# A hybrid encoder layer on one core: stores moved from ScalarE to GpSimd, first input pieces in other tiles, a later residual load

## The chip, the core and the metric

The kernel runs on one core of a Trainium2 chip. The core has TensorE (PE in the profile; its weight loads are PEld), VectorE (DVE), ScalarE (ACT), GpSimd (POOL) and SyncE (SP), which here only issues DMAs. Each engine takes its instructions in its own order and waits on semaphores for the others. SBUF holds the tiles, PSUM the results of matmuls (eight banks of 128 x 512 f32), and larger arrays lie in DRAM. The metric is the device time of one execution in microseconds (us), the median of several.

## What is computed

One layer of a bidirectional encoder in float32: 2048 positions, width 1024. Cut to what matters here:

```python
u = rms_norm(x); proj = u @ w_in                       # 1024 -> 3600 columns
hy = conv3(proj[:, :1536])                             # v, x1, x2, 512 channels each
z, g1, g2 = hy                                         # Hyena: two long convolutions
for o, gate in enumerate((g1, g2)):
    conv = irfft(rfft(z, 2 * L) * spec[:, o])[:L]      # spec from a small sine network
    z = gate * (conv + z * skip[o])
qk = silu(conv3(proj[:, 1536:2560]))                   # mLSTM: 4 heads of 128, two directions
y_ml = sigmoid(o_pre) * (mlstm(q, k, v, gates) + flipped)
h = x + concat(group_norm(z), group_norm(y_ml)) @ w_out
h = h + cross_attention(rms_norm(h), rms_norm(mem))    # 256 memory rows, 4 heads
h = h + square(relu(rms_norm(h) @ w1)) @ w2            # 1024 -> 4096 -> 1024
return rms_norm(h)
```

## The kernel before

All large products are made in three matmuls: each operand is split into a rounded part and its remainder (`split`, L368, one ScalarE and one VectorE instruction), and `mm3` multiplies high x high (L357), high x low (L360) and low x high (L361). They write the four PSUM banks called `mm`. The long convolutions, filters and mLSTM steps use the other four, called `hy`.

The program is one list of instructions, and a planner (`schedule_with_timeline_sim`) puts each engine's part in order by a model of the times. Where the source says `behind(ins)`, the planner places `ins` after the last product made so far; no semaphore comes of it. `weave(a, b, wa, wb)` alternates two parts of the program: each `yield n` adds n to its part's account, and the part with the smaller account over its weight goes on.

The stages up to the attention, in the order of time:

- **Projection** (`sweep` and `natural`). `sweep` makes 128 columns by 512 positions per product (`yield 5.5`), leaves them in tiles P (L789), applies the short convolution in tiles cv (L797 to L802) and stores the turned result into the arrays hy, qt, kt and kn. `natural` makes the value, output gate and mLSTM gate columns (eight row blocks per 256 columns): ScalarE moves the bank into a staging tile st (L892, L894; three buffers, two row blocks each) and issues the store into vd or od (L897). For the gates VectorE adds the bias into sg (L900; two buffers of 128 x 16), and SyncE stores it into gt (L901), once per row block, sixteen times.
- **Filters** (`filters`), woven into the sweeps, in a pool of their own (`f_sb`). The matrix f1 (128 x 64) is loaded there. `front` stores the filter spectra into the arrays fs (L339). When the filters are done the pool closes, and the pool `h_sb` of the Hyena part is laid over the same memory: ten tiles `a` of 128 x 1024, five tiles b, and f1 once more, loaded again (L931).
- **Hyena** (`hyena`), woven with the rest of the projection at weights 329 and 445. First `load1` fetches a piece of hy in four DMAs (L938) into a tile `a`, for eight pieces; `spectrum(0, ...)` turns each by sixteen small matmuls over four hy banks (`beside`, L173 and L186), ScalarE and VectorE copy the banks out (L997), and the two halves are stored into zs (L339): one from ScalarE's queue, one from SyncE's. Then per block i: load of zs and fs (L918), matmul by dm (L955 for the filter, L1029 for the data), the complex product with ScalarE (L1031, L1032), VectorE (L1033, L1035) and GpSimd (L1034), matmul by em (L986), copy to gs (L987) and store into zg from ScalarE's queue (L988, 64 of them). Then `load3` reads zg and the gate rows (L339, L973), the last small matmuls follow, and VectorE multiplies by the gate (L1050). All this runs twice (o = 0, 1); for o = 0 the result goes through `spectrum(1, ...)`, for o = 1 it is normed on VectorE and GpSimd (L1059 to L1065) and stored into yh (L1067).
- **Backward mLSTM states** (`states`): load of va (L1183), weighting on GpSimd (L1195), matmul L1199, update L1205, store.
- **Memory products** (`memproj`), beside the first mLSTM steps: `project` (L709, copied by L711) and `keys` (L726) or `values` (L738), whose banks ScalarE copies into staging tiles st (L716) and stores from its own queue into gd (L728) and vw (L740).
- **mLSTM and attention.** At its start attention reads yh and ym rows, turns them on TensorE (L1478) and splits them (L368); `residual` (L1507) loads the 1 MB halves of x into acc. The mLSTM step reads va too (L1183) and weights it on ScalarE (L1193).

After the attention comes the feed-forward part to the end; nothing of the change lies there. The small pool `i_sb` holds, among others, two tiles xn of 128 x 1024, used by `row_stats` near the start and by the memory loads later.

Of the kernel before, what the change touches and what calls it, by code (L numbers as in the profile page):

```python
# [10 lines left out]
F32 = mybir.dt.float32  # L11
# [117 lines left out]
class Prog:  # L129
# [102 lines left out]
    def filters(self):  # L232
# [1 line left out]
        sd = [self.dram(f"fs{o}", (16, 64, 4, CH)) for o in range(2)]  # L234
        sb, ta, tb = self.fsb, self.ta, self.tb
        if True:
            fw, hid, f1 = self.f_w, self.f_hid, self.f_f1
            nc.sync.dma_start(out=fw, in_=a["fw"])
            w1, w2, w3 = fw[0:66, 0:128], fw[:, 128:256], fw[:, 256:1280].rearrange("p (o c) -> p o c", o=2)
            par = self.par[:, 128:132]  # L240
# [100 lines left out]
    def filters_open(self):  # L341
        self.fes = ExitStack()
        self.fsb = self.fes.enter_context(self.tc.tile_pool(name="f_sb", bufs=1))
        self.fsb.tile([128, 32], F32, name="f_even")
        self.f_w = self.fsb.tile([128, 1280], F32, name="fw")
        self.f_hid = self.fsb.tile([128, 16, 128], F32, name="hid")
        self.f_f1 = self.fsb.tile([128, 128], F32, name="f1")[:, 0:64]

    def ta(self):
        return self.fsb.tile([128, 2, CH], F32, tag="a", name="a", bufs=7)  # L350
# [77 lines left out]
    def inproj_open(self, es):  # L428
        nc, tc, a = self.nc, self.tc, self.a
        self.d_hy = self.dram("hy", (3, L, CH))  # L430
        self.d_qt = self.dram("qt", (4, 128, L))
        self.d_kt = self.dram("kt", (4, 128, L))
        self.d_kn = self.dram("kn", (L, CH))
        self.d_vd = self.dram("vd", (L, CH))
        self.d_od = self.dram("od", (L, CH))
        self.d_gt = self.dram("gt", (L, 16))
        sw = self.isw = es.enter_context(tc.tile_pool(name="i_w", bufs=1))
        for tag, n, bufs in (("cv", 1088, 2), ("wn", 544, 4)):
            for _ in range(bufs):
                sw.tile([128, n], F32, tag=tag, name=tag, bufs=bufs)  # L440
        self.ist = es.enter_context(tc.tile_pool(name="i_st", bufs=1))
        sb = self.isb = es.enter_context(tc.tile_pool(name="i_sb", bufs=1))
        self.xin = ExitStack()
        xp = self.xin.enter_context(tc.tile_pool(name="x_sb", bufs=1, side="right"))
        self.xh = xp.tile([128, 8, 1024], F32R, name="xh")
        self.xl = xp.tile([128, 8, 1024], F32R, name="xl")
        xp.tile([128, 56], F32, name="x_even")
        small = sb.tile([128, 448], F32, name="small")
        self.carry = small[:, 0:340].rearrange("p (c t) -> p c t", c=20)
        self.rx, self.rm = small[:, 340:356], small[:, 356:358]  # L450
        win = a["w_in"][0]
        tr = [(win[:, 256 * c:256 * c + 256], 256) for c in range(10)]
        nat = [(win[:, 2560 + 256 * c:2816 + 256 * c + 16 * (c == 3)], 256 + 16 * (c == 3)) for c in range(4)]
        hs = [slice(256 * h, 256 * h + 256) for h in range(4)]
        first = [(a[w][0][:, h], 256) for w in ("xa_wk", "xa_wv") for h in hs]
        second = [(a["xa_wq_t"][h, :], 1024) for h in hs] + [(a["xa_wo"][0][h, :], 1024) for h in hs]
        mem = first[:1]
        for i in range(8):
            mem += first[i + 1:i + 2] + second[i:i + 1]
        items = tr[:4] * 2 + tr[4:] + [nat[c] for c in (3, 0, 1, 2, 3)]  # L460
        items += [tr[c] for c in (4, 5, 8, 9)] + nat[:2] + tr[6:8] + nat[2:3]
        self.items, self.mem_items = items, mem
# [231 lines left out]
    def memproj(self):  # L694
# [24 lines left out]
        def keys(h, t):  # L719
            q = next(self.mst)  # L720
            for i2 in range(4):
                p = self.mm().rearrange("p (i t) -> p i t", i=2)
                for i in range(2):
                    ds = slice(256 * i2 + 128 * i, 256 * i2 + 128 * i + 128)
                    for m in range(2):
                        mul(p[:, i], q[:, m, ds], t[:, m], start=m == 0, stop=m == 1)  # L726
                cs = slice(256 * (h % 2), 256 * (h % 2) + 256)
                nc.scalar.dma_start(out=gd[h // 2, :, 2 * i2:2 * i2 + 2, cs], in_=staged(p))  # L728

        def values(h, t):  # L730
            o_ = next(self.mst)
            for mt in range(2):
                ms = slice(128 * mt, 128 * mt + 128)
                for d in range(2):
                    ds = slice(512 * d, 512 * d + 512)
                    p = self.mm()
                    for m in range(2):
                        mul(p, t[:, m, ms], o_[:, m, ds], start=m == 0, stop=m == 1)  # L738
                    o = staged(p.rearrange("p (i t) -> p i t", i=2))
                    nc.scalar.dma_start(out=vw[2 * d:2 * d + 2, :, 2 * h + mt].rearrange("i p c -> p i c"), in_=o)  # L740

        t = project()
        for i in range(8):
# [117 lines left out]
    def natural(self, hf, tiles, after=None, at=4):  # L861
# [3 lines left out]
        for c2 in tiles:  # L865
# [3 lines left out]
            for t in range(8):  # L869
# [24 lines left out]
                    nc.scalar.activation(so, p[:, :256], AF.Sigmoid)  # L894
                if t % 2:
                    dst = (self.d_vd if c2 < 2 else self.d_od)[r0 - 128:r0 + 128, 256 * (c2 % 2):256 * (c2 % 2) + 256]
                    nc.scalar.dma_start(out=dst.rearrange("(t p) c -> p t c", p=128), in_=st)  # L897
                if c2 == 3:
                    sg = sb.tile([128, 16], F32, tag="sg", name="sg", bufs=2)
                    nc.vector.tensor_tensor(sg, p[:, 256:272], self.gb, ALU.add)  # L900
                    nc.sync.dma_start(out=self.d_gt[r0:r0 + 128], in_=sg)  # L901

    def hyena(self, es):
        nc, tc, a = self.nc, self.tc, self.a
# [18 lines left out]
        def ta():  # L923
            return sb.tile([128, 2, CH], F32, tag="a", name="a", bufs=10)
# [1 line left out]
        def tb():  # L926
            return sb.tile([128, CH], F32, tag="b", name="b", bufs=5)

        f1 = sb.tile([128, 128], F32, name="f1")[:, 0:64]
        e2 = sb.tile([128, 64], F32, name="e2")[:, 0:32]  # L930
        nc.sync.dma_start(out=f1, in_=a["c_f1"])  # L931
        nc.sync.dma_start(out=e2, in_=a["c_e2"])
        ghy = self.bcast(sb, a["hy_norm_g"], CH, "ghy")
        def load1(j2):
            z = ta()
            js = slice(2 * j2, 2 * j2 + 2)
            for q in range(4):
                nc.sync.dma_start(out=z[phase[q]], in_=hy[0, q, :, js])  # L938
            return z
# [44 lines left out]
        def back(m, i, em, y, gs, dst):  # L984
            pg = self.hy()
            nc.tensor.matmul(pg, em[:, m], y, start=True, stop=True)  # L986
            nc.scalar.copy(gs[:, m], pg)  # L987
            nc.scalar.dma_start(out=of_block(dst, i, m), in_=gs[:, m])  # L988

        def spectrum(o, j2, z):  # L990
            st = [ta() for h in range(2)]
# [4 lines left out]
                for h in range(2):  # L996
                    (nc.vector.tensor_copy if h else nc.scalar.copy)(st[h][:, i], pp[2 * h + i])  # L997
            for h in range(2):
                self.by_phase(nc.sync if h else nc.scalar, sds[o], j2, h, st[h])

        q, fq = [load1(0), load1(1)], []
        yield 52
        self.strict = True
        for j2 in range(8):
            yield 3.5
            if j2 < 6:
                q.append(load1(j2 + 2))
            else:
                fq.append(load_filter(0, j2 - 6))
            spectrum(0, j2, q.pop(0))  # L1010
# [426 lines left out]
    def attention(self, es):  # L1437
# [65 lines left out]
        for c in range(4):  # L1503

            def residual(h):
                src = a["x_t"].rearrange("(k p) t -> p k t", p=128)[:, 4 * h:4 * h + 4, 512 * c:512 * c + 512]
                nc.sync.dma_start(out=acc[:, 4 * h:4 * h + 4], in_=src)  # L1507

            ssum = A.tile([128, 512], F32, tag="ssum", name="ssum", bufs=2)

# [679 lines left out]
```

## Time and profile before

| what | value |
|---|---|
| median of three runs | 3098.77 us (3090.32 to 3103.11) |
| profiled execution, its own time | 3100.22 us |
| its span, first to last instruction | 3098.5 us |
| mean granted clock of TensorE | 0.984 |
| DMA queue of SyncE | 407012 packets, 546.46 MB |
| DMA queue of ScalarE | 37380 packets, 57.79 MB |
| DRAM read, written | 401.70 MB, 202.41 MB |

How to read the rows shown below. A stretch (window) row gives the busy time of each engine between two times, the clock that TensorE was granted (1.00 is full), the share of the sixteen DMA engines' time and what they moved. A row of waits names the engine, the tile it writes and its line, what ended the wait, and then the total, the number of times and the longest, in us. A row of one line or tile gives the shortest, median and longest instruction in ns, and the first and last start. In timeline and chain rows the first number is the start and the second the length; in the chain a DMA's length is the time from its issue until what waited for it could go on. SPq and ACTq are the DMA queues of SyncE and ScalarE.

### The profile page before, as it was taken

The numbers are of one execution on the slowest core, as the hardware profiler recorded it, in microseconds if no ns is written. First come the engines' busy times: TensorE is split into PE (matmuls) and PEld (weight loads), VectorE is DVE, ScalarE is ACT, GpSimd is POOL, SyncE is SP. The second block draws the span as 40 slices with busy tenths as digits, with TensorE's granted clock in tenths as the row PEclk, the third lists the DMA queues.
The fourth block names the chain that finished last, engine by engine and source line by source line (L and its number), as shares of the span: only waits on it lengthen the run. The fifth ranks groups of instructions, "written<-read, shape, count | busy, mean of one in ns | idle before, by whom it ended". The sixth has DMA issues, their size and how long they took to land.

```text
span 3098.5 us, 44022 instructions
## 1 busy us (share of the span) xinstructions
PE 2989.6 (96%) x14799; PEld 2371.5 (77%) x14799; DVE 1945.6 (63%) x3442; ACT 1494.4 (48%) x2930; POOL 1121.0 (36%) x798
## 2 busy tenths in 40 slices
PE   9999899999999898999999999999999999999998
PEld 7666566776577676888888888888888888888876
DVE  8855365547745445877664666557555686566695
ACT  6443356534744235565544465556555543333335
POOL 0111012200222333333132336766466375344653
PEclk9999999999999999999999999999999999999999
DMA  6555578586767996465476556657544565354434
GB/s 223 188 191 175 198 238 250 181 268 201 241 212 217 315 303 195 152 200 167 150 245 217 188 185 226 209 179 241 196 153 151 179 213 175 110 165 119 155 102 163
DMA packets 444618, 607.06 MB, mean 196 GB/s; under 512 B 39262, under 2 KB 249054, under 8 KB 443368
## 3 DMA queue, kind: packets, MB, share of 16 engines
q1 hardware_dynamic: 407012, 546.46, 55.0%
q10 hardware_dynamic: 37380, 57.79, 5.5%
q8 instruction: 117, 1.92, 0.3%
q14 instruction: 109, 0.89, 0.1%
HBM read 401.70 MB, written 202.41 MB: 195 GB/s over the span
## 4 chain that ended last, share of the span: by engine, by line
PE 81%; DMA 9%; DVE 6%; issue 2%; ACT 1%; SPq 1%; POOL 0%; ACTq 0%; DVEq 0%; POOLq 0%
PE mm L357 17%; PE mm L361 17%; PE mm L360 17%; PE hy L357 6%; PE hy L361 6%; PE hy L360 6%; PE hy L173 2%; PE hy L1029 2%; PE hy L986 2%; PE mm L955 2%; DMA a<-zg 1%; PE mm L709 1%; PE hy L1321 1%; DMA xt<-in_x_t_dram 1%; PE hy L1323 1%
## 5 line engine op out<-in xcount | busy, mean ns | idle before, releaser
L1689 ACT CAST ah<-w 128x512 fp32r<-128x512 f32 x284 | 176.6, 623 | 302.1 <-PE hy L360 157.0
L1690 DVE TENSOR_TENSOR bl<-wr,bh 128x512 fp32r<-128x512 f32 x213 | 240.8, 1135 | 126.5 <-ACT bh L1689 126.4
L368 DVE TENSOR_TENSOR wl<-wn,wh 128x512 fp32r<-128x512 f32 (+1 forms) x296 | 215.7, 773 | 101.2 <-ACT wh L368 101.2
L357 PE MATMUL mm<-xh,wh 128*128 128x512 f32 x640 | 267.2, 419 | 3.2 <-ACT st L201 1.4
L360 PE MATMUL mm<-xl,wh 128*128 128x512 f32 x640 | 258.0, 403 | 4.5 <-DVE xl L368 4.4
L1034 POOL TENSOR_TENSOR b<-b,a 128x512 f32<-128x512 f32 x64 | 87.1, 1362 | 481.4 <-ACT b L1032 240.1
L361 PE MATMUL mm<-xh,wl 128*128 128x512 f32 x640 | 257.6, 403 | 0.0
L1689 ACT CAST bh<-wr 128x512 fp32r<-128x512 f32 x232 | 143.6, 621 | 229.9 <-PE mm L361 171.3
L1690 DVE TENSOR_TENSOR al<-w,ah 128x512 fp32r<-128x512 f32 x236 | 214.6, 910 | 55.1 <-ACT ah L1689 55.1
L361 PE MATMUL mm<-bh,al 128*128 128x512 f32 x576 | 224.1, 392 | 4.1 <-DVE al L1690 4.1
L357 PE MATMUL mm<-bh,ah 128*128 128x512 f32 x576 | 226.2, 393 | 0.5 <-DVE acc L1851 0.4
L360 PE MATMUL mm<-bl,ah 128*128 128x512 f32 x576 | 225.1, 391 | 0.0
L368 ACT CAST wh<-wn 128x512 fp32r<-128x512 f32 (+1 forms) x296 | 164.7, 620 | 105.4 <-PE mm L361 50.1
L360 PE MATMUL mm<-act,wh 128*128 128x512 f32 x512 | 201.9, 394 | 0.0
L357 PE MATMUL mm<-act,wh 128*128 128x512 f32 x512 | 199.4, 396 | 1.0 <-ACT wh L368 0.9
L361 PE MATMUL mm<-act,wl 128*128 128x512 f32 x512 | 199.6, 392 | 0.0
L357 PE MATMUL hy<-bh,ah 128*128 128x512 f32 x448 | 175.2, 391 | 0.0
L360 PE MATMUL hy<-bl,ah 128*128 128x512 f32 x448 | 174.6, 390 | 0.0
L361 PE MATMUL hy<-bh,al 128*128 128x512 f32 x448 | 174.4, 390 | 0.0
L357 PEld LDWEIGHTS mm<-xh,wh 128*128 128x128 f32 x640 | 122.4, 191 | 58.2 <-issue 24.3
L360 PEld LDWEIGHTS mm<-xl,wh 128*128 128x128 f32 x640 | 122.8, 192 | 47.4 <-issue 16.3
L357 PE MATMUL mm<-wh,xh 128*128 128x256 f32 (+1 forms) x512 | 157.4, 307 | 0.5 <-ACT st L894 0.5
(380 smaller groups left out, 8077.8 us busy)
## 6 DMA issues: line engine op xcount, KB each, us to landing
wr<-hc SPq DMA_DIRECT2D x224, 256.0 KB
w<-in_ff_w_dram SPq DMA_DIRECT2D x172, 256.0 KB
hc<-wn SPq DMA_DIRECT2D x128, 256.0 KB
wn<-in_w_in_dram SPq DMA_DIRECT2D x100, 256.0 KB
hc<-q SPq DMA_DIRECT2D x96, 256.0 KB
fs<-a SPq DMA_DIRECT2D x32, 512.0 KB
a<-fs SPq DMA_DIRECT2D x64, 256.0 KB
a<-zs SPq DMA_DIRECT2D x64, 256.0 KB
```

What stands on the lines that cost most here:

```text
L173: b = self.nc.tensor.matmul(*products[-1], start=True, stop=True)
L357: first = mm(ps, lh, rh, start=start, stop=False)
L360: mm(ps, lh, rl, start=False, stop=False)
L361: self.last = mm(ps, ll, rh, start=False, stop=stop)
L368: both = (self.nc.scalar.copy(hi, src), self.nc.vector.tensor_tensor(lo, src, hi.bitcast(F32), ALU.subtract))
L709: mul(p[:, m], w[:, k, ms], mt[k // 4][:, k % 4], start=k == 0, stop=k == 7)
L955: nc.tensor.matmul(pp, dm[:, m], t[:, m], start=True, stop=True)
L986: nc.tensor.matmul(pg, em[:, m], y, start=True, stop=True)
L1029: nc.tensor.matmul(pp, dm[:, m], t[:, m], start=True, stop=True)
L1034: nc.gpsimd.tensor_tensor(xt, xt, hi[:, m], ALU.mult)
L1689: self.nc.scalar.copy(hi, src)
L1690: eng.tensor_tensor(lo, src, hi.bitcast(F32), ALU.subtract)
```

## The change

```diff
 filters:
-            fw, hid, f1 = self.f_w, self.f_hid, self.f_f1
+            fw, hid, f1 = self.f_w, self.f_hid, self.f1
 filters_open:
-        self.fsb.tile([128, 32], F32, name="f_even")
-        self.f_f1 = self.fsb.tile([128, 128], F32, name="f1")[:, 0:64]
 inproj_open:
+        self.f1 = sb.tile([128, 64], F32, name="f1")
 memproj, keys and values:
-                nc.scalar.dma_start(out=gd[...], in_=staged(p))
+                nc.gpsimd.dma_start(out=gd[...], in_=staged(p))
-                    nc.scalar.dma_start(out=vw[...], in_=o)
+                    nc.gpsimd.dma_start(out=vw[...], in_=o)
 natural:
-                    nc.scalar.dma_start(out=dst.rearrange("(t p) c -> p t c", p=128), in_=st)
+                    nc.gpsimd.dma_start(out=dst.rearrange("(t p) c -> p t c", p=128), in_=st)
                 if c2 == 3:
-                    sg = sb.tile([128, 16], F32, tag="sg", name="sg", bufs=2)
-                    nc.vector.tensor_tensor(sg, p[:, 256:272], self.gb, ALU.add)
-                    nc.sync.dma_start(out=self.d_gt[r0:r0 + 128], in_=sg)
+                    if t == 0:
+                        sg = sb.tile([128, 8, 16], F32, tag="sg", name="sg", bufs=1)
+                    nc.vector.tensor_tensor(sg[:, t], p[:, 256:272], self.gb, ALU.add)
+                    if t == 7:
+                        dst = self.d_gt[1024 * hf:1024 * hf + 1024]
+                        nc.sync.dma_start(out=dst.rearrange("(t p) g -> p t g", p=128), in_=sg)
 hyena:
-        f1 = sb.tile([128, 128], F32, name="f1")[:, 0:64]
+        f1 = self.f1
-        nc.sync.dma_start(out=f1, in_=a["c_f1"])
 load1:
-            z = ta()
+            z = ta() if j2 > 1 else self.isb.tile([128, D], F32, tag="xn", name="z", bufs=2).rearrange("p (j c) -> p j c", j=2)
 back:
-            nc.scalar.dma_start(out=of_block(dst, i, m), in_=gs[:, m])
+            nc.gpsimd.dma_start(out=of_block(dst, i, m), in_=gs[:, m])
 spectrum:
-                self.by_phase(nc.sync if h else nc.scalar, sds[o], j2, h, st[h])
+                self.by_phase(nc.sync if h else nc.gpsimd, sds[o], j2, h, st[h])
 the eight pieces of spectrum(0, ...):
-            yield 3.5
+            yield 4.2
 attention, residual:
-                nc.sync.dma_start(out=acc[:, 4 * h:4 * h + 4], in_=src)
+                d = nc.sync.dma_start(out=acc[:, 4 * h:4 * h + 4], in_=src)
+                if c == 0:
+                    self.behind(d)
```

f1 is loaded once, into the small pool, and read by the filters and by Hyena. The first two pieces that Hyena reads lie in the two tiles xn; the other six in tiles `a`, as before. All stores that ScalarE issued in `natural`, `memproj`, `back` and `spectrum` are issued by GpSimd. The gates of eight row blocks are gathered in one tile and stored by one DMA per half of the positions. The eight pieces of the first spectrum weigh 4.2 in the weave, where they weighed 3.5. The first chunk's residual loads stand behind the last product made before them.

More of the change, by code (lines that the diff above doesn't have):

```diff
@@ L727, in keys @@
                 cs = slice(256 * (h % 2), 256 * (h % 2) + 256)
-                nc.scalar.dma_start(out=gd[h // 2, :, 2 * i2:2 * i2 + 2, cs], in_=staged(p))
+                nc.gpsimd.dma_start(out=gd[h // 2, :, 2 * i2:2 * i2 + 2, cs], in_=staged(p))
         def values(h, t):
@@ L739, in values @@
                     o = staged(p.rearrange("p (i t) -> p i t", i=2))
-                    nc.scalar.dma_start(out=vw[2 * d:2 * d + 2, :, 2 * h + mt].rearrange("i p c -> p i c"), in_=o)
+                    nc.gpsimd.dma_start(out=vw[2 * d:2 * d + 2, :, 2 * h + mt].rearrange("i p c -> p i c"), in_=o)
         t = project()
```

## Prediction

> **What bounds the kernel now.** I read the page's busy times first, then the stretches by stage, then what TensorE waited for, then single waits in the timeline.
>
> ```profile
> PE 2989.6 (96%) x14799; PEld 2371.5 (77%) x14799; DVE 1945.6 (63%) x3442; ACT 1494.4 (48%) x2930; POOL 1121.0 (36%) x798
> ```
>
> TensorE works 96% of the span, and the change removes no matmul. What can be won is its 109 us of idle time and the time in which its clock is down. The stretches show where that is (columns: stretch, its length, busy us and count of PE, PEld, DVE, ACT, POOL, then granted clock, DMA share, GB/s):
>
> ```profile
> 350.00:430.00 80.00, 64.61 (x337) 43.05 (x336) 32.60 (x51) 33.97 (x55) 0.00 (x0) 0.87 0.80 275
> 430.00:640.00 210.00, 205.43 (x1136) 153.15 (x1135) 124.79 (x194) 129.77 (x231) 42.79 (x32) 0.99 0.71 217
> 640.00:760.00 120.00, 105.72 (x657) 74.78 (x657) 70.67 (x155) 44.53 (x76) 3.84 (x2) 0.93 0.76 242
> 760.00:1020.00 260.00, 248.96 (x1279) 183.68 (x1278) 160.51 (x323) 142.00 (x240) 62.77 (x48) 0.99 0.74 225
> 1020.00:1120.00 100.00, 86.18 (x445) 69.60 (x444) 44.50 (x143) 23.60 (x56) 38.06 (x32) 0.93 0.96 311
> 1120.00:1210.00 90.00, 77.54 (x391) 58.28 (x390) 45.86 (x152) 43.32 (x147) 24.94 (x20) 0.92 0.78 260
> 1900.00:3098.00 1198.00, 1178.29 (x5245) 974.32 (x5243) 762.29 (x989) 539.42 (x934) 670.85 (x462) 0.99 0.52 169
> ```
>
> Between 350 and 1210 us, where every edit acts, PE is idle 71.6 us (860 less the six busy times); in the 1198 us of the feed-forward stage, which no edit touches, 19.7. The waits of PE name the causes (us in total, times, longest):
>
> ```profile
> PE hy L173 <- DMA a<-hy: 11.7, 1, 11.7
> PE hy L1478 <- DVE act L368: 9.1, 1, 9.1
> PE mm L726 <- ACT kt L711: 7.6, 2, 3.9
> PE hy L173 <- ACT a L997: 5.4, 2, 3.7
> PE hy L173 <- DVE a L1050: 5.3, 2, 4.6
> PE hy L986 <- DVE b L1035: 4.5, 2, 2.4
> ```
>
> Each long one also lowers the clock behind it. Pairs of ten-microsecond stretches around four of them, same columns:
>
> ```profile
> 350.00:360.00 10.00, 0.97 (x4) 0.45 (x3) 5.09 (x7) 6.85 (x11) 0.00 (x0) 0.73 0.92 319
> 360.00:370.00 10.00, 7.33 (x32) 4.68 (x33) 1.29 (x2) 1.08 (x2) 0.00 (x0) 0.59 0.89 255
> 390.00:400.00 10.00, 6.30 (x45) 2.99 (x44) 8.31 (x14) 7.03 (x11) 0.00 (x0) 0.78 0.81 260
> 400.00:410.00 10.00, 10.00 (x51) 7.28 (x50) 1.82 (x4) 2.52 (x5) 0.00 (x0) 0.88 1.02 398
> 670.00:680.00 10.00, 5.38 (x28) 4.13 (x26) 2.93 (x7) 3.21 (x7) 0.00 (x0) 0.94 0.62 217
> 680.00:690.00 10.00, 10.00 (x54) 5.98 (x55) 2.56 (x5) 1.66 (x3) 0.00 (x0) 0.71 0.89 260
> 1190.00:1200.00 10.00, 2.08 (x15) 1.34 (x13) 4.18 (x21) 3.98 (x19) 3.79 (x4) 0.89 0.87 307
> 1200.00:1210.00 10.00, 7.80 (x41) 7.47 (x42) 8.55 (x22) 5.38 (x14) 0.00 (x0) 0.60 0.75 247
> ```
>
> I price a stall as idle time plus busy time times the missing clock. At 350: 9.0 + 2.7 idle and 7.33 x 0.41 = 3.0, together 14.7 us. At 390: 3.7 and 6.30 x 0.22 + 10 x 0.12 = 2.6, together 6.3. At 670: 4.6 and 0.3 + 2.9, together 7.8. At 1190: 7.9 + 2.2 and 0.2 + 3.1, together 13.4. These four cost 42 us of 3100.
>
> **The change part by part.** *First input pieces.* The timeline of SyncE's queue and the chain at the first stall:
>
> ```profile
> 351.07 2.69 DMA fs<-a
> 356.72 7.37 SPq L938 DMA_DIRECT2D a<-hy  x11
> ```
>
> The pieces a<-hy go into tiles that lie where the filter tiles lay; the last filter store lands at 353.8, and eleven piece loads leave in one burst from 356.7. The data in hy are far older. In the small pool the first eight loads (two tiles of four) need only the two slots xn, which the row statistics used last near the start, so they can leave before 350. The single f1 tile drops one 32 KB load and its wait from the same place. PE then goes from the last projection product into the spectrum at once. What is late next are the copies L997, whose targets still lie on filter tiles until 353.8; PE meanwhile has the next product, and four mm banks. The third piece now heads the burst. I take all of the stall: -14.7 (without the clock part, -11.7).
>
> *Yield 3.5 to 4.2.* A projection product yields 5.5 and the weave weighs 445 to 329, so one spectrum per 3.5 x 445 / 329 / 5.5 = 0.86 products becomes one per 1.03. Below one, two spectra sometimes follow without a whole product between them, and the second finds its four hy banks not yet copied out by L997: the wait of 3.7 at 390. I take -6.3 (0 at worst). In return all later Hyena steps stand 8 x 0.7 x 445 / 329 = 7.6 units, some 1.4 products, later against the projection, and Hyena ends after it. Memory products cover that, but in a stage whose DMA share is 0.96. Between 0 and +7.6 us; I take +2, as PE had work in most of that stage.
>
> *Stores leave ScalarE.* By the loops of the source these are 64 zg, 16 zs, 32 vd and od, 16 gd, 16 vw: 144 instructions. Two rows of waits in 340 to 700 and one of 700 to 1210:
>
> ```profile
> DVE sg L900 <- DMA gt<-sg: 8.7, 4, 3.7
> ACT st L894 <- DMA a<-zg: 8.7, 1, 8.7
> ACT kt L711 <- DMA gd<-o: 7.8, 1, 7.8
> ```
>
> ScalarE stood 8.7 us at an od store until a load of SyncE's had landed, though the data of the store were its own: I read it so that an issue waits for a place among the transfers under way, and all that follows on ScalarE waits with it. Gate rows: sg has two buffers, each row's store waits in SyncE's queue, and VectorE stood 8.7 us for it; L1050, which PE awaited at 675, was behind. One tile and one store per eight rows ends that, and takes 14 of 16 issues off SyncE. The stalls around 650 to 690 are worth 7.8 plus the small waits of 1.7 (the rest of L997) and 0.7 (the rest of L1050): 10.2 at most, 0 at least since DMA is nearly full there; I take -6. In the memory products PE waited 7.6 us for L711 behind gd stores. Weights must still arrive at the same DMA rate, so -3 (0 to -7.6).
>
> What the stores do on GpSimd no row of before shows; it issues no DMA. The nearest rows:
>
> ```profile
> L988 ACTq DMA_DIRECT2D zg<-a x64: 524/526/613, 438.6 to 963.4; - x64
> L339 SPq DMA_DIRECT2D a<-zg x32: 319/400/1585, 626.0 to 1080.6; - x32
> L728 ACTq DMA_DIRECT2D gd<-o x16: 366/366/406, 1056.7 to 1117.6; - x16
> L1034 POOL TENSOR_TENSOR b<-b,a x64: 1266/1296/2045, 433.3 to 955.4; 128x512 f32<-128x512 f32 x64
>   DVE b L1035: 22.0, 36
> POOL va L1195 <- DMA va<-vd: 82.1, 11, 12.3
> ```
>
> The zg store waits for ScalarE's copy L987, and behind it on GpSimd stands the next L1034, for which L1035, then the matmul L986, wait. Today VectorE waits 22.0 us for L1034, of which PE saw 4.5: a fifth. A store that holds GpSimd 0.53 us (as L988) adds 64 x 0.53 / 5 = +7; at 1.6 (the longest issue row) +20; 0 if it fits into GpSimd's idle time. I take +7, the like instruction's row. GpSimd is idle in the two spectrum stages (0.00 and 3.84 us busy), so zs, od and vd stores cost nothing there. Four times a stage's last stores are read at once by the next (zs, then zg, for both orders): issue 0.33 to 1.6, so 0 to +4.4; I take +2. In the memory products a gd store can stand behind L1195, which waited up to 12.3 us for va. L728's 16 stores are 61 us apart first to last, 4 us each, and three staging tiles cover about 12 of it; +3, at most +12.3.
>
> The Trainium skill, "DMA: Bandwidth & Descriptors", section "Issuing engine by pattern", advises SyncE for simple stores, since GpSimd's descriptors are made by software; its table gives about 1 us to the first byte against 0.6. By that the four hand-overs cost 4 x 0.4 = 1.6 us, an estimate from that page, in place of my 2. No run here shows it.
>
> *Later residual.* At 1190 the attention stage's own loads stand in the way:
>
> ```profile
> 1190.51 0.92 SPq L1507 DMA_DIRECT2D acc<-in_x_t_dram  x2
> 1192.02 7.56 DMA va<-vd
> ```
>
> Two loads of 1 MB leave just ahead of va, which takes 7.56 us; ScalarE waits for va in front of the casts L368 that PE needs. The edit puts the residual behind the half products in the planned order; nothing waits for it in hardware. If it moves past va, 2 MB at the row's 307 GB/s are 6.8 us. Other loads remain, and a gap of 4 us still lowers the clock at 390, so I take -4.5 (0 to -13.4).
>
> **Sum.** -14.7 - 6.3 - 6 - 3 - 4.5 = -34.5; +2 + 7 + 2 + 3 = +14; net -20.5. The profiled execution took 3100.2 us (span 3098.5, 1.7 around it): 3079.7. It ran 1.4 above the median of 3098.77, so the median should be **3078**. With all gains and no costs (-52.2) it would be 3047; with the first gain at -11.7 alone and all costs (44.3) 3131.
>
> **Rivals.** *Stalls move* (0.26): the order of all engines is planned anew, and a later Hyena meets the x reload and the memory weights elsewhere. For: DMA share 0.96 at 1020, so freed engines wait for data. Against: the 350 stall is a pure release wait with nothing behind it. Then only it pays and the rest cancels: 3098.8 - 14.7 = 3084, up to 3098 if the piece loads stay late in SyncE's queue, which would be the change not doing what it says.
>
> *GpSimd becomes the queue* (0.12): each zg store holds it while L1034 stands behind, and PE, which takes its instructions in order, sees the whole hold instead of a fifth. For: L1034 is on the chain of every Hyena step. Against: GpSimd is 20% busy in 430 to 640 (42.79 of 210). With a hold of 1.3 us, one instruction of GpSimd's own, that is 83 us: -34.5 + 2 + 2 + 3 + 83 = +56, or 3154. It is slower by over 0.5% from a hold of (34.5 - 7 + 15.5) / 64 = 0.67 us on. The Trainium skill, "SBUF — State Buffer", in its box on the trap "DVE blocks DMA", holds that GpSimd cannot write descriptors while VectorE has the shared port; VectorE is busy 62% of 760 to 1020 (160.51 of 260), so it would lengthen just this hold. No run here shows it yet.
>
> **How the numbers follow.** Half a per cent, 15.5 us, is about what a measurement of this kernel can tell from no change. Forecast 0.62 (below 3083.3, its upper end with less than half of the smaller gains); stalls move 0.26; GpSimd 0.12. Those are also the chances of faster, same and slower. Range 3052 to 3108: below it need nearly all gains at no cost (0.06), above it lies the third case; between 3098 and 3108 the first gain is eaten by GpSimd at moderate holds.
>
> **What would show it.** Right: no wait L173 <- a<-hy near 350, piece loads before the last fs store; no wait of L173 for L997; no wait of L900 for gt; no ACT wait ended by another queue's DMA at L894 or L711; va landing in about 4 us near 1190. Wrong: waits L986 <- L1035 well above 4.5 us; POOL rows with stores over 0.67 us and L1034 behind them; new PE waits for a<-zs or a<-zg; a longer stretch 1020 to 1120.

## The result and the profile after

| kernel | median us | runs | ratio to before (95% interval) |
|---|---|---|---|
| before | 3097.53 (3090.32 to 3103.11) | 4 | |
| after | 3075.28 (3073.00 to 3076.67) | 4 | 0.9931 (0.9914 to 0.9948) |

The change makes the kernel 22.3 us faster, and the interval lies wholly beyond half a per cent. The profiled executions took 3100.22 and 3074.8 us, 25.4 apart. Lines of the kernel after stand at most three off those of before (L986 is now L987, L726 L725, L711 L710, L1029 L1030, L997 L998, L1478 L1479).

The busy times on the page of the kernel after:

```profile
PE 2981.7 (97%) x14799; PEld 2367.8 (77%) x14799; DVE 1947.8 (63%) x3442; ACT 1491.4 (49%) x2930; POOL 1213.7 (39%) x942
```

The matmuls are the same 14799. PE is idle 91.4 us of its span of 3073.1, where it was 108.9: 17.5 of the 25.4 us. The rest is PE's busy time, 7.9 us shorter at a mean clock of 0.988 for 0.984. GpSimd has 144 instructions more, the stores, and is 93 us busier.

The stretches of the kernel after, columns as in the prediction:

```profile
350.00:430.00 80.00, 72.47 (x392) 50.98 (x393) 38.90 (x62) 37.84 (x61) 5.77 (x9) 0.98 0.89 297
640.00:760.00 120.00, 105.00 (x622) 70.52 (x622) 69.02 (x196) 43.18 (x77) 8.36 (x12) 0.93 0.79 249
760.00:1020.00 260.00, 253.52 (x1322) 190.32 (x1321) 159.37 (x289) 146.24 (x254) 97.39 (x102) 1.00 0.77 235
1020.00:1120.00 100.00, 91.35 (x451) 68.44 (x451) 41.82 (x126) 20.93 (x44) 47.91 (x47) 0.97 0.98 333
1120.00:1210.00 90.00, 76.11 (x423) 62.61 (x422) 55.98 (x181) 52.30 (x185) 40.18 (x36) 0.91 0.68 221
```

Read them against the rows of before. 350 to 430 gained 7.9 us of PE work, 760 to 1020 4.6, 1020 to 1120 5.2. The stretch 640 to 760 gained nothing (105.00 against 105.72, the same clock 0.93), and 1120 to 1210 lost 1.4. The six largest waits of PE between 340 and 1240 in the kernel after (total, times, longest):

```profile
PE hy L1030 <- DMA a<-zs: 8.8, 3, 4.4
PE mm L725 <- ACT kt L710: 5.8, 2, 4.2
PE hy L1479 <- DVE act L366: 4.8, 1, 4.8
PE hy L1322 <- DVE ht L1356: 4.3, 1, 4.3
PE hy L1134 <- DVE ends L1129: 3.6, 1, 3.6
PE hy L173 <- DVE a L998: 3.4, 1, 3.4
```

The 11.7 us for a<-hy are gone. Of the rows shown, two have no counterpart before: L1134 for `ends` (the mLSTM gate scan on VectorE, near 710) and L1322 for `ht` (an mLSTM step near 1158). To see where along the way the time was won, take the last output product of Hyena, Hyena's last gate product, the last memory product and the attention's additions, first in the kernel before (each row: shortest, median, longest in ns, then first and last start in us):

```profile
L986 PE MATMUL hy<-b,em x128: 590/592/1018, 436.5 to 962.2; 128*128 128x512 f32 x128
L1050 DVE TENSOR_TENSOR a<-hy,a x32: 669/681/693, 635.5 to 1101.7; 128x512 f32<-128x512 f32 x32
L738 PE MATMUL mm<-wm,kt x64: 592/592/594, 1124.5 to 1183.6; 128*128 128x512 f32 x64
L1513 DVE TENSOR_TENSOR acc<-mm,acc x64: 654/686/693, 1230.2 to 1838.7; 128x512 f32<-128x512 f32 x64
```

and in the kernel after:

```profile
L987 PE MATMUL hy<-b,em x128: 590/592/922, 430.1 to 952.2; 128*128 128x512 f32 x128
L1051 DVE TENSOR_TENSOR a<-hy,a x32: 677/684/694, 639.9 to 1105.4; 128x512 f32<-128x512 f32 x32
L737 PE MATMUL mm<-wm,kt x64: 592/592/594, 1093.7 to 1145.6; 128*128 128x512 f32 x64
L1516 DVE TENSOR_TENSOR acc<-mm,acc x64: 654/685/693, 1204.7 to 1813.9; 128x512 f32<-128x512 f32 x64
```

All of the gain is there when the attention's additions begin (25.5 us), 10.0 of it by the last output product. The memory products end 38.0 us earlier, but Hyena's last gate product comes 3.7 us *later*. That pair of numbers is the clue to what follows: one part of the change works against the others.

### The profile page after: what moved, and what is told of

The parts are those of the page before. It is cut to its first block, busy times and chain, and to the rows that moved or that the text cites. A ratio compares the mean times of both kernels' runs of the same rounds, so it can differ in the third digit from the quotient of the medians.

```text
span 3073.1 us, 44126 instructions
## 1 busy us (share of the span) xinstructions
PE 2981.7 (97%) x14799; PEld 2367.8 (77%) x14799; DVE 1947.8 (63%) x3442; ACT 1491.4 (49%) x2930; POOL 1213.7 (39%) x942
## 4 chain that ended last, share of the span: by engine, by line
PE 82%; DMA 7%; DVE 5%; issue 2%; ACT 2%; POOL 1%; SPq 1%; DVEq 0%; ACTq 0%; POOLq 0%
PE mm L355 17%; PE mm L358 17%; PE mm L359 17%; PE hy L359 6%; PE hy L355 6%; PE hy L358 6%; PE hy L173 2%; PE hy L1030 2%; PE mm L956 2%; PE hy L987 1%; DMA va<-vd 1%; DMA a<-zg 1%; PE hy L1322 1%; PE hy L1324 1%; PE mm L825 1%
## 5 line engine op out<-in xcount | busy, mean ns | idle before, releaser
L331 POOL TENSOR_TENSOR b<-b 128x512 f32<-128x512 f32 x32 | 48.1, 1504 | 293.3 <-DVE b L330 273.7
```

What stands on the lines that cost most here:

```text
L331: nc.gpsimd.tensor_tensor(b, f, b, ALU.subtract)
```

## The experiments

Twelve kernels ran, in three groups on three chips, each timed against runs of the kernel before on the same chip; so the ratios are compared, and "us below before" is 1 less the ratio, times 3097.5. Names with `a_` undo or alter a part of the kernel after, names with `b_` add a part to the kernel before.

| run | edit | median us | ratio (95% interval) | us below before |
|---|---|---|---|---|
| after | all five parts | 3075.28 | 0.9931 (0.9914 to 0.9948) | 21.4 |
| a_noxn | first pieces undone | 3079.75 | 0.9950 (0.9938 to 0.9963) | 15.5 |
| a_act | all stores on ScalarE | 3084.90 | 0.9963 (0.9950 to 0.9976) | 11.5 |
| a_zgact | only stores zg on ScalarE | 3079.77 | 0.9937 (0.9925 to 0.9948) | 19.5 |
| a_res | residual undone | 3077.34 | 0.9945 (0.9932 to 0.9957) | 17.0 |
| a_gate | gate store undone | 3070.22 | 0.9915 (0.9902 to 0.9928) | 26.3 |
| a_y35 | yield 3.5 | 3066.91 | 0.9916 (0.9900 to 0.9931) | 26.0 |
| a_y28 | yield 2.8 | 3063.78 | 0.9891 (0.9878 to 0.9904) | 33.8 |
| a_y28_gate | yield 2.8, gate store undone | 3064.01 | 0.9886 (0.9873 to 0.9899) | 35.3 |
| b_xn | first pieces alone | 3087.01 | 0.9970 (0.9955 to 0.9984) | 9.3 |
| b_pool | stores on GpSimd alone | 3085.47 | 0.9967 (0.9955 to 0.9979) | 10.2 |
| b_two | these two together | 3072.66 | 0.9917 (0.9904 to 0.9930) | 25.7 |
| b_y42 | yield 4.2 alone | 3096.61 | 0.9989 (0.9977 to 1.0002) | 3.4 |

### First input pieces: a_noxn and b_xn

a_noxn, in `load1` of the kernel after:

```diff
-            z = ta() if j2 > 1 else self.isb.tile([128, D], F32, tag="xn", ...)
+            z = ta()
```

> The changed kernel with one part undone: the first two input tiles go back into tiles a, which lie on the filter tiles (f1 stays shared). Theory A (each stall is worth its idle time and the clock behind it): PE's wait L173 <- a<-hy near 350 is back at 9 to 12 us, the piece loads leave in one burst near 355, and the time is 12 to 15 us above the changed kernel, about 3088 (ratio to before 0.997). Theory B (only this stall pays, the rest of the change cancels itself): the whole gain of 22 us goes with it, 3097 (ratio 1.000).

PE's wait at the first spectrum came back in full:

```profile
PE hy L173 <- DMA a<-hy: 12.0, 1, 12.0
```

The price at the end did not. At the last output product the run stands 8.2 us behind the kernel after (960.4 against 952.2), at the first attention addition 6.3 (1211.0 against 1204.7), in the ratios 5.9, with intervals that overlap. Theory B, by which the whole gain would go, is out; theory A named the wait rightly and priced it some two times too high for this kernel, whose later stages give part of it back.

b_xn, the same tiles and the shared f1 in the kernel before:

```diff
-            z = ta()
+            z = ta() if j2 > 1 else self.isb.tile([128, D], F32, tag="xn", ...)
-        f1 = sb.tile([128, 128], F32, name="f1")[:, 0:64]
-        nc.sync.dma_start(out=f1, in_=a["c_f1"])
+        f1 = self.f1
```

> The kernel before with one part of the change alone: the first two input tiles in the two slots xn and the shared f1. Yield 3.5, stores on ScalarE, gate rows and residual as before. Theory A (stall price, 14.7 us all kept): first input product near 351 with no wait for a<-hy, time 14 us below before, 3082 (0.995). Theory D (given back on the way: undone alone in the changed kernel it cost a wait of 12 us but only 8 us by the last output product of the convolution and some 4 at the end): the same 12 us at 350, 3 to 6 us at the end, 3090 to 3093 (0.998 to 0.999), the stall near 390 gone or halved as in the run with yield 3.5, Hyena's last step before 1090, and the memory products' waits for kt unchanged.

9.3 us, with an interval of 5 to 14: below A's 14 and above D's 3 to 6, though the interval touches both. In the trace the lead isn't given back on the way here: the first input product comes at 351.7 for 362.7, the last output product 11.2 us earlier (951.0), the last attention addition 12.3 (1826.4). So alone the edit is worth about the wait that it removes, 11.7 us, and not its clock as well. The stall near 390 did not go: in 380 to 390 PE was busy 3.70 us at clock 0.65.

### Stores off ScalarE: a_act, b_pool, a_zgact

a_act puts all five groups back on ScalarE's queue; b_pool does the opposite edit in the kernel before:

```diff
-                nc.gpsimd.dma_start(out=gd[...], in_=staged(p))
+                nc.scalar.dma_start(out=gd[...], in_=staged(p))
...
```

> The changed kernel with all five groups of stores issued by ScalarE again. Theory A, by my terms: the gains of the stores at 640 to 690 and in the memory products (6 + 3) go, the costs on GpSimd (7 + 2 + 3) go too: 3 us below the changed kernel, 3072; the wait of L987 for L1036 falls if the store hold on GpSimd costs anything, ACT waits ended by another queue's DMA at L896 and L710 are back, and the first memory output products stand 7 us late for kt. Theory B: within 3 us, no pattern. Theory C (the stores are where the 15 us between 960 and 1230 come from, because ScalarE no longer stands behind the memory stage's weight loads): 10 to 15 us above, 3085 to 3090, with the last memory product 15 or more us later.

9.9 us slower than the kernel after by the ratios, at the lower edge of theory C's 10 to 15, and mine (3 us faster) fell. It also says where. The last output product stands as in the kernel after (951.4 against 952.2), the last memory product 11.3 us later (1156.9 against 1145.6; C had asked for 15). The timeline of ScalarE in a_act, within the first memory products; the brackets give idle time before, and what ended it:

```profile
1025.64 0.58 ACT L715 COPY o<-mm 128x512 f32<-128x512 f32 x1
1032.38 0.38 ACTq L727 DMA_DIRECT2D gd<-o  x1
1032.80 0.58 ACT L715 COPY o<-mm 128x512 f32<-128x512 f32 x1 [6.58 <-DMA wm<-in_xa_wq_t_dram]
...
1040.74 0.57 ACT L715 COPY o<-mm 128x512 f32<-128x512 f32 x1
1047.35 0.37 ACTq L727 DMA_DIRECT2D gd<-o  x1
1047.76 0.58 ACT L710 COPY kt<-mm 128x512 f32<-128x512 f32 x1 [6.45 <-DMA a<-zg]
```

The staging copy o ends at 1026.2, so the data of the store are there; yet the store leaves at 1032.38, in the moment when a weight load of SyncE's queue lands. What follows on ScalarE begins behind it. At 1041 to 1048 the same happens with kt behind, which PE needs for its next products.

The trace also tells what the store waits for. It lists for each issue the semaphores that it waits for and the one that its own landing will add to. SyncE and ScalarE share eight such semaphores for all their DMAs (1977 and 194 in a_act), and nearly every issue first waits until the DMA that used its semaphore before has landed. The store at 1032.38 takes the semaphore of the weight load wm that SyncE had issued at 1023.25; the last of that load's sixteen updates came at 1032.30, and the wait was over at 1032.32. All 16 gd stores of a_act have such a wait, and 14 of the 16 ended 0.02 us after the landing of a DMA of SyncE's. The store doesn't need that DMA's data; it only has to wait for the semaphore. In the kernel after the 144 stores of GpSimd have eight semaphores of their own, 18 stores each, and none of their waits ended with a landing: the store before had always landed by then.

In total over the eight copies kt (idle time of ScalarE before them, and what ended it):

```profile
  DMA a<-zg: 12.6, 2
  PE mm L708: 11.3, 2
  DMA kn<-kn: 8.5, 1
```

In the kernel after the same copies wait for nothing but their own matmuls:

```profile
  PE mm L708: 22.4, 4
```

> The kernel before with the five groups of stores issued by GpSimd and nothing else. Theory C (the gain of the stores lies in the memory products, where ScalarE's copies kt and the staging copies stood behind stores that wait for other queues' transfers): same landmarks until 960 within 3 us, no ACT wait ended by another queue's DMA at L711, wait L726 <- kt below 6 us, last memory product 10 us or more earlier, time 8 to 11 us below before, 3086 (0.997). Theory A, by my terms (gains 9, costs 12): 3 us above before, with more wait of L986 for L1035 than 4.5 us. Theory B: within 3 us of before.

10.2 us below before: the size as theory C said. The place is C's in the main. The last output product, the last memory product, the attention's additions and PE's wait for kt in b_pool:

```profile
L986 PE MATMUL hy<-b,em x128: 590/592/1002, 435.8 to 951.9; 128*128 128x512 f32 x128
L738 PE MATMUL mm<-wm,kt x64: 592/592/595, 1108.7 to 1172.0; 128*128 128x512 f32 x64
L1513 DVE TENSOR_TENSOR acc<-mm,acc x64: 653/686/693, 1210.3 to 1819.9; 128x512 f32<-128x512 f32 x64
PE mm L726 <- ACT kt L711: 1.1, 1, 1.1
```

Against before the two products are 10.3 and 11.6 us earlier and the first addition 19.9. (Its profiled execution, 3080.31, was the fastest of eight and 19.9 us shorter than that of before, so the leads are larger than the 10.2 us of the ratio.) The 10.3 us at the last output product miss C's 3 us until 960, but they are in part a matter of order: up to 1020 us PE was busy 963.9 us in b_pool and 963.8 before. The stretch 1020 to 1120 is where PE does more (92.08 us against 86.18, at clock 0.98 for 0.93), and its wait for kt falls there from 7.6 us to 1.1. So in both kernels the held stores cost their time mainly in the memory products.

a_zgact asks what the stores cost on GpSimd. Only the 64 zg stores, behind which L1035 stands, go back:

```diff
-            nc.gpsimd.dma_start(out=of_block(dst, i, m), in_=gs[:, m])
+            nc.scalar.dma_start(out=of_block(dst, i, m), in_=gs[:, m])
```

> The changed kernel with only the 64 stores zg issued by ScalarE again, the other 80 on GpSimd. Theory A, my term for the hold of 0.53 us on GpSimd (7 us on PE): last output product L987 some 5 to 7 us earlier than in the changed kernel, 3068 to 3070. Theory N (GpSimd has room, the wait of L987 for L1036 did not grow: 2.1 us against 2.8 with all stores on ScalarE): the last L987 within 3 us, time within 3 us of the changed kernel, 3073 to 3078.

Theory N held: no gain (0.9937 against 0.9931, its interval within the other), the last output product at 954.0 against 952.2. The hold itself is in the row of the 64 stores of the kernel after:

```profile
L989 POOL DMA_DIRECT2D zg<-a x64: 530/553/631, 437.2 to 953.7; - x64
```

0.553 us each, as I had assumed, but it lies in GpSimd's idle time: VectorE's wait for GpSimd's product, in the kernel after

```profile
  POOL b L1035: 14.2, 32
```

was 22.0 us before, and is 17.7 in a_zgact. It did not grow with the stores.

### The yield: a_y35, a_y28, b_y42

```diff
-            yield 4.2
+            yield 3.5
```

(a_y28: 2.8; b_y42: 3.5 to 4.2 in the kernel before.)

> The changed kernel with yield 3.5 for 4.2 in the first spectrum loop. Theory A: the stall near 390 (a wait of L173 for the copies L998) is back, 4 to 6 us more by 430; Hyena ends earlier, which gives 2 back: 2 to 5 us above the changed kernel, 3077 to 3080. Theory B: the stall only moves, time within 2 us of the changed kernel; a stall near 390 that is back while the first input product of the convolution stays where it is would speak for B.

> The changed kernel with yield 2.8 for 4.2 (3.5 gave 3067). Theory G (an earlier end of Hyena is what pays: its tail, not the memory products, sets the attention's start): the tail's last gate product L1051 comes another 20 to 35 us earlier, but then the memory products end last, so the gain stops: 3062 to 3068. Theory A (below one spectrum per product the second spectrum waits for its hy banks): stalls of L173 for L998 of 4 us and more in 360 to 430, with the clock down, 3072 or more.

> The kernel before with yield 4.2 and nothing else. Theory M (in the kernel before the memory products end last, 80 us after Hyena's last gate product, so a later Hyena is covered there, and the stall near 390 goes): L1050 last at about 1110 or later, wait of L173 for L997 gone, time 2 to 6 us below before, 3091 to 3095. Theory K (the parts add: 4.2 cost 8 us in the changed kernel, so it costs as much here): 3103 to 3106.

The yield was a part that I had counted as a gain. Undone in the kernel after it makes it *faster*, by 4.6 us at 3.5 and by 12.4 at 2.8. Theories A and B of a_y35 had it slower or the same. The interval at 3.5 overlaps that of the kernel after, the one at 2.8 does not, and a_y28_gate repeats it. a_y28 in two stretches:

```profile
640.00:760.00 120.00, 111.91 (x639) 74.24 (x638) 81.06 (x210) 54.57 (x95) 17.10 (x21) 0.99 0.76 244
1120.00:1210.00 90.00, 81.83 (x439) 66.49 (x439) 61.86 (x184) 54.98 (x187) 43.39 (x37) 0.94 0.66 213
```

Against the kernel after PE works 6.9 us more in the first (and at 0.99 for 0.93) and 5.7 in the second. These are the places of the two new waits, L1134 for `ends` and L1322 for `ht`. And b_y42, in the kernel before, has both, where the kernel before has neither (PE's waits between 440 and 1240):

```profile
PE hy L1321 <- DVE ht L1355: 4.3, 1, 4.3
PE hy L1133 <- DVE ends L1128: 4.3, 1, 4.3
```

Over all fourteen profiles, the seven with yield 4.2 all have the wait for `ends` (3.6 to 5.1 us) and the wait for `ht` of L1356 (2.4 to 5.1), whatever their other parts; of the seven with 3.5 or 2.8 none has either. Both come with a later Hyena. Near 710 its last spectra then meet the gate scan, which sits in one place of VectorE's order: VectorE is busy 9.33 and 9.72 us of 710 to 720 and 720 to 730 in the kernel after, and PE 2.99 of the first. At the end the memory products, which should stand beside Hyena's tail and the first mLSTM steps, are used up before: they end 40.2 us after Hyena's last gate product in the kernel after (1145.6 less 1105.4). In a_y28 that product stands here

```profile
L1051 DVE TENSOR_TENSOR a<-hy,a x32: 677/682/692, 622.6 to 1068.0; 128x512 f32<-128x512 f32 x32
```

and the memory products end at 1145.8, the same as after, 77.8 us behind it. In b_y42 the distance is 40.2 (1167.1 less 1126.9), before it was 81.9. That the short distance makes the wait for `ht` is read from these profiles; no run changes the distance alone.

Theory G held in the time (3063.78), but not in how it came about: from 3.5 to 2.8 the tail moved hardly any further (1069.7 to 1068.0, where G had asked for 20 to 35 us); the output products moved, which end at 927.5 for 937.5. Theory A's stall did not appear at 2.8 (waits for L998 of 1.4 and 1.2 us), though waits of 2.9 and 2.6 for the pieces a<-hy did. For b_y42, theory K (it costs as much here) fell, and M's gain of 2 to 6 us can't be told from nothing: 3.4, with an interval from -0.6 to 7.1. M's reason, that the memory products cover a later Hyena, fell too: the distance is 40.2 there as well, and the wait for `ht` is there. What b_y42 gives in exchange are waits that the kernel before has and the kernel after doesn't: L173 for L997 (5.4 us, gone), L173 for L1050 (5.3, now 1.6). PE's idle time is 107.9 us (span 3095.8 less 2987.9 busy) against 108.9. The stalls moved. In the changed kernel those waits are short at 3.5 too (a_y35: 1.3 us for L998, none for L1051), so there the later Hyena has its price and nothing to pay for. That comparison rests on the traces; between 3.5 and 4.2 alone the times differ by less than their intervals.

### Residual, gate store, and the two parts together: a_res, a_gate, a_y28_gate, b_two

a_res takes `self.behind(d)` out of `residual`:

```diff
-                if c == 0:
-                    self.behind(d)
```

> The changed kernel with the first residual loads not put behind the half products. Theory A: the two 1 MB loads stand ahead of va again, va takes 7 us or more in place of 3.3, and the attention's start is 4 to 7 us later: 3079 to 3082. Theory B: the stall is there anyway (L1479 still waits 4.8 us for L366 in the changed kernel), time within 2 us of it.

The chain of a_res just ahead of the attention, and one of PE's waits:

```profile
1156.81 0.38 SPq L1508
1157.24 0.49 SPq L1508
1157.83 7.75 DMA ym<-ht
1173.80 3.12 DMA va<-vd
```

```profile
PE hy L1200 <- ACT ht L1336: 6.1, 2, 5.7
```

The two residual loads stand ahead again, but what is slow behind them is now the store ym (7.75 us), not va, which takes 3.12 us as in the kernel after (3.28). PE's wait for the copy behind ym, the second row, was 0.5 us in the kernel after. The attention's first product comes 6.0 us later (1176.3 against 1170.3), as theory A said; in the time it is 4.3 us, which the intervals don't separate from none.

a_gate puts the old code of the gates back, one store per row block:

```diff
-                    if t == 0:
-                        sg = sb.tile([128, 8, 16], F32, tag="sg", name="sg", bufs=1)
-                    nc.vector.tensor_tensor(sg[:, t], p[:, 256:272], self.gb, ALU.add)
-                    if t == 7:
-                        dst = self.d_gt[1024 * hf:1024 * hf + 1024]
-                        nc.sync.dma_start(out=dst.rearrange("(t p) g -> p t g", p=128), in_=sg)
+                    sg = sb.tile([128, 16], F32, tag="sg", name="sg", bufs=2)
+                    nc.vector.tensor_tensor(sg, p[:, 256:272], self.gb, ALU.add)
+                    nc.sync.dma_start(out=self.d_gt[r0:r0 + 128], in_=sg)
```

> The changed kernel with one gate store per row block again (sg of 16 numbers, two buffers, 16 stores on SyncE). Theory A: VectorE waits for the store of gt again, some 8 us in all near 640 to 700, PE sees 2 to 6 us of it: 3077 to 3081. Theory E (the four other parts undone one at a time add up to 8 us of the 22; the rest is here): 10 us or more above the changed kernel, 3085 or more. Theory F (parts overlap: the late pieces and the low yield together made the stall at 390, each alone does not): within 3 us of the changed kernel, 3075 to 3078.

> The changed kernel with yield 2.8 and one gate store per row block. Theory P (the single gate store costs something of its own, as the 5 us between a_gate and the changed kernel would have it): 3057 to 3060. Theory Q (the gate rows are worth nothing either way, the 5 us are scatter between runs): 3062 to 3066, as a_y28.

VectorE waits for the store again, 7.3 us in all, and PE sees nothing of it: PE's busy time in 640 to 760 is 105.12 us against 105.00. The 5 us by which a_gate stands below the kernel after are not the gate store's price, as a_y28_gate has it: 0.9886 against 0.9891 (theory Q). Theories A and E are out; F's 3 us fit only within the intervals.

b_two is the kernel before with the edits of b_xn and b_pool.

> The kernel before with two parts together: the first input tiles in xn with the shared f1, and the five groups of stores on GpSimd; yield 3.5, gate rows and residual as before (so it is the run a_y35 less gate and residual). Theory K (the parts add: 9.8 and 11.4 below before alone): 3075 to 3078. Theory L (with PE earlier at 350 and the memory products freed, each makes the other worth more, and gate and residual are worth 0 to 3 us): 3067 to 3071, as a_y35 within 4 us.

25.7 us below before, at least as much as all five parts. The two single gains add to 19.5, and the ends of their intervals to 11.5 and 27.8, so b_two (21.7 to 29.7) may be their plain sum or a little more: K and L stay undecided, and the median fell between their figures. What it settles: these two parts carry the whole gain. The gate store and the residual, which a_y35 has besides, change nothing in the ratios at yield 3.5 (0.9917 and 0.9916); the one profile of each would have it otherwise (spans 3076.2 and 3065.2; 4.5 us more PE work in 640 to 760 in a_y35), and whether one of the two is worth something there stays open.

The version that beats both kernels is a_y28 (or a_y28_gate): 0.9891 of before, 12.4 us below the kernel after by the ratios.

## Why the prediction was right, and where it was not

The forecast of 3078 lies 2.7 us above the median, and the net of -20.5 us beside the measured 22.3. The terms behind it are another matter. The first pieces and the residual came out with the sign that was forecast, and the gate store and the hold of the zg stores had no weight. The stores as a whole, which cost at least 3 us net in the sum, gained 10, and the yield, which gained 4 there, gained nothing that can be told from none.

| step | forecast us | measured us |
|---|---|---|
| first pieces | -14.7, or -11.7 without the clock | -9.3 alone (-5 to -14), -5.9 by undoing |
| yield 4.2 | -6.3 + 2 | -3.4 alone (+0.6 to -7.1); in the changed kernel +4.6 against 3.5, +12.4 against 2.8 |
| stores, with their part of the -6 | gains up to 9, costs 12 | -10.2 alone, -9.9 by undoing |
| of these, the hold of the zg stores | +7 | 0 (-1.9 by the medians of the ratios, inside both intervals) |
| gate store, with its part of the -6 | part of -6 | 0 at yield 4.2 and 2.8 (5 us the other way by one ratio, not repeated) |
| later residual | -4.5 | -4.3 by undoing, 0 not excluded |

**First pieces.** Right, mechanism and place: z<-hy is loaded at 213 to 217, far ahead of the last filter store, and the wait is gone. The row that shows it in the kernel after:

```profile
L939 SPq DMA_DIRECT2D z<-hy x8: 303/403/421, 213.1 to 216.5; - x8
```

Mis-sized was the clock part, 3.0 us on top of 11.7, of which nothing shows.

**Yield.** The step that failed is "Memory products cover that ... I take +2, as PE had work in most of that stage". PE had work there *before*, with the memory products ending 81.9 us behind Hyena's last gate product. The yield itself halves that distance, from both ends (b_y42: the gate product 25.2 us later, the memory products 16.5 earlier), and then nothing stands beside the last steps. I had moved one side of the weave and left the other where it was. And I priced the gain against the profile of before, where waits stood that other parts of the change end as well. In the kernel after the stall at 390 did go (PE busy 10.00 us at clock 1.00 in 390 to 400), but PE then waited 3.3 us near 420 for the hand-over a<-zs, and 3.6 near 710.

**Stores.** The row `ACT st L894 <- DMA a<-zg` was read rightly as an issue by ScalarE that waits for a transfer of another queue, and ending such waits is the largest gain beside the first pieces. The reason given, "a place among the transfers under way", was not right: the od store ahead of that row waited for its own semaphore, which a load a<-zg of SyncE's had used before it. Mis-sized were the memory products, at 3 us, which a_act shows as 11.3 at their end, and the costs on GpSimd. That vd and od stores cost nothing because GpSimd is idle in the spectrum stages was a misreading, since 30 of these 32 stores fall into the two stages of the output products in the kernel after. They hold GpSimd some 0.74 us each, over the 0.67 of the sign list, and yet PE's wait there did not grow. Taking "a fifth" of each hold from the ratio of two waits (4.5 of 22.0) had no ground: the wait of L987 for L1036 went down, from 4.5 to 2.1. The third cost, gd behind L1196, was not tried by itself; nor were the hand-overs, beyond this: the waits for a<-zs total 8.8 us after, and 11.4 in a_act, with those stores on ScalarE; those for a<-zg total 2.8 us after, 1.5 in a_act and 0.6 before. Of the signs of being right, no wait of L710 was ended by a DMA, and va landed in 3.28 us; but PE waited 3.4 us for L998 (L997 before) near 720, right behind the wait for `ends`.

**Gate store.** The 8.7 us of VectorE were real and the edit ends them, but at yield 4.2 and 2.8 they were on nobody's path. "L1050, which PE awaited at 675, was behind" was an order of two rows, not a cause.

**Residual.** In size as forecast, though none isn't excluded, and the transfer that waits behind the loads is ym.

**The rivals.** "GpSimd becomes the queue" fell with the hold of 0.553 us, under the 0.67 that it needed. The Trainium skill, "SBUF — State Buffer", box on the trap "DVE blocks DMA", speaks of VectorE's two-port operations alone, which a float32 copy from SBUF to SBUF starts, so I should not have counted all of VectorE's busy time. Here VectorE was busy 159.37 of 260 us between 760 and 1020, mostly with tensor-tensor operations and copies out of PSUM, and the longest of the 64 stores took 0.631 us, so the runs hardly test the box. "Stalls move" fell as a forecast of the time, but describes the yield well: 3.7 us at 390 became 3.3 at 420, 3.6 at 710 and 4.3 at 1158.

So the total was right in part by luck, since errors of opposite sign met. The costs on GpSimd did not come (12 us). Against that the first pieces gave 5 to 9 us less than forecast, the gate store gave nothing, and the yield gained nothing in the changed kernel, where I had it gain 4 (at 2.8 it runs 12 us faster).

## What to carry to other kernels

When an engine both computes and issues stores, look at the gap between the end of the copy and the issue of its store in that engine's timeline: if a foreign DMA ends the gap, the store is being held and holds the work behind it. Then look up which semaphore it waits for: if that is one that it shares with another queue, an engine with idle time there and semaphores of its own can take the issue. Price an edit that shifts one part of the program against another (a weave weight, a yield) on both ends of the shift and with the other edits in, since the work that covers it moves too. And a wait of an engine that isn't the bound is only worth something if an instruction that the bound waits for can be followed to it.

## What the runs showed of the hardware

That issues of GpSimd are not held where those of ScalarE are was not expected. The traces put it down to the semaphores that this program gives to its DMAs, as told under a_act, and not to a trait of the engines. In a_act the first ten gd stores left 2.7 to 6.2 us behind the copy before them; in the kernel after what GpSimd waits for ahead of its 16 gd stores is its own data, and each holds it longer than ScalarE's 0.366 us did:

```profile
L727 POOL DMA_DIRECT2D gd<-o x16: 725/748/765, 1027.5 to 1091.2; - x16
  ACT o L715: 6.3, 4
  ACT brm L208: 1.8, 1
```

The transfers of these gd stores still take their time, a median of 7.1 us from issue to landing, and the three staging tiles wait for them (20.8 us in all on ScalarE; among PE's waits none is for o). Two things stay open. SyncE's issues wait for the shared semaphores too, for 150.0 us in all between 340 and 1210 before and 102.8 in b_pool, and no run tells how much of the gain comes from its earlier loads. And no run leaves the stores on ScalarE with semaphores of their own, which by this account would end the holds as well.
